# In each slot of the attention loop, the inverse's product moved to directly behind the scores, the maxima behind it

## The chip, the cores and the metric

The kernel runs on one core of a Trainium2 chip. The time is the device time of one execution in microseconds (us). Each engine (TensorE or PE, VectorE or DVE, ScalarE or ACT, GpSimd or POOL) works through its own list of instructions, and semaphores hold an instruction back until what it needs is done. SyncE (SP) issues the transfers. Matmul results go to PSUM, whose eight banks are shared out by hand in this kernel.

## The reference

One mixer layer of a diffusion backbone, 2048 latent tokens behind 256 context tokens, width 1024. One projection feeds two groups of heads, whose outputs are gated, concatenated, projected and added to the residual:

```python
rw_l, _ = rwkv_branch(rwkv_prep(u_sh, *rw_p), ctx_states, ...)   # RWKV-7: a delta-rule state, both directions
k, v = mla_keys_values(u_mla, kv_g, w_ukv, rot)                  # 8 heads, low-rank keys and values
q = mla_queries(u_mla, q_g, w_uq, rot)
o = block_attention(q, concat([k, kc]), concat([v, vc]))         # softmax over 2304 keys
x = x + gate * (concatenate([rw_l, o * silu(g_mla)]) @ w_out)
return rms_norm(x, final_g)
```

## The kernel before

The kernel has an input phase (projections, until about 1000 us), a short phase for queries, keys and values, and then the loop that the change touches, `attention`, from 1186 us to the end. It runs 16 **jobs**, one for each pair of heads and tile of 512 queries (`hp`, `qt`). A job has nine **macros** (`m` = 0 to 8), a macro four **slots** (`j` = 0 to 3) and a fifth call `side(4)` without scores. A slot does this on PE, in this order:

- **scores**: three matmuls of 512 columns (L1438 to L1440) into one buffer `bs`; ACT takes the exponential of it (L1442, tile `pt`), POOL adds that to `acc` (L1447);
- **maxima** for the next job's softmax: none to five matmuls (L1318) of 512 or 256 columns, each into a `bs` buffer of its own, each reduced on DVE to one column (L1319, tile `m`). They are handed out by a budget of columns (`due`, `rate`) in macros 1 to 7, and the list is emptied in macro 8;
- **side(j)**: while the RWKV branch lasts, `rw.slot`, which takes the inverse of one chunk one step on. A step is a product of 8 to 17 small matmuls (L328, L331, L334) into a `bx` buffer and its eviction on DVE or ACT. In slot 3 of every third macro `rw.slot` also issues the transposes of a chunk (L287). When the branch is done, `side` calls `late`, which issues steps of the output phase (`post`, `out_tiles`), most of them DVE work.

`bs` has three PSUM banks, which scores and maxima share, and `bx` two. Behind the four slots a macro issues the product with the values (`pv`, L1465, eight matmuls) and a larger piece of the RWKV branch (`tiled`). By the macro's number modulo 3 that is `chain1` and the next scores of the branch (L407, L308, L417; macros 0, 3, 6), `chain2` (L433; macros 1, 4, 7) or `chain3` and `chain4` (L447, L463; macros 2, 5, 8).

`chain2` needs the tile `Rf`, the inverse's last eviction (L394, DVE). Ahead of it on DVE stands the scaling of the next chunk's keys (L251, tile `x`): SP loads `x` behind the scores of `chain1` (L245), ACT takes two exponentials of it (L247, L248), then DVE multiplies (L251).

PE's order is the order in which the code is written (`manual_schedule` for PE). The orders of DVE, ACT, POOL and SP, and which of the three banks a `bs` tile gets, are set when the program is built, by a scheduler that estimates when each operation becomes ready; on the chip they are fixed. Jobs 0, 1, 2, 4, 5, 6, 8 and 9 are alike up to the names of the banks (called regular below). Jobs 3 and 7 prepare maxima for another pair of heads, with keys of 256 columns from a buffer `kx`. The branch ends in job 10; jobs 11 to 15 run `late`.

Of the kernel before, what the change touches and what calls it, by code (L numbers as in the profile page):

```python
# [468 lines left out]
class Kern:  # L469
# [864 lines left out]
    def attention(self, top, es, right, k, q, load_q, maxima, sets, pieces):  # L1334
        nc, tc, rw = self.nc, self.tc, self.rw
        L, CT, NT = self.L, self.CT, self.NT
        QW = min(512, L)
        NQ, NK, NQS = L // QW, NT // P, QW // P
        KW, NP = 512, len(pieces)
        kp = es.enter_context(tc.tile_pool(name="kp", bufs=1))  # L1340
        sets[1] = es.enter_context(tc.tile_pool(name="qb", bufs=1))
        pp = es.enter_context(tc.tile_pool(name="pp", bufs=2))

        KS, VS = [], []
        for j, (o, w) in enumerate(pieces):
            kt = kp.tile([97, 2, 2, w], F32R, name=f"kt{j}")
            for e in range(2):
                nc.sync.dma_start(kt[64:97, e].bitcast(F32), self.s_krr[:, :, o:o + w].rearrange("s p t -> p s t"))
            KS.append(kt)
            VS.append(kp.tile([P, w // P, P], F32, name=f"vt{j}"))  # L1350

        def load_kv(hp, j):
            o, w = pieces[j]
            for e in range(2):
                nc.sync.dma_start(KS[j][0:64, e].bitcast(F32),
                                  self.s_kn[:, hp, 64 * e:64 * e + 64, o:o + w].rearrange("s p t -> p s t"))
            nc.sync.dma_start(VS[j], self.s_vm[o:o + w, hp * P:(hp + 1) * P].rearrange("(j p) c -> p j c", p=P))

        def finish(hp, qt, oo, acc, last):

            cols = slice(qt * QW, (qt + 1) * QW)
            ob = pp.tile([P, QW], F32, name="ob", bufs=1)
            nc.scalar.copy(ob, oo)
            yield 1
            dn = self.bank("s")
            for e in range(2):
                nc.tensor.matmul(dn[64 * e:64 * e + 64, 0:QW], self.ones[:, 0:64], acc[e], start=True, stop=True)
            gr = pp.tile([P, 2, QW], F32, name="gr", bufs=1)
            g, rc = gr[:, 0], gr[:, 1]
            nc.scalar.copy(rc, dn[:, 0:QW])  # L1370
            nc.sync.dma_start(g, self.s_g[4 + hp][:, cols])
            yield 1
            for c in range(0, QW, P):
                nc.vector.reciprocal(rc[:, c:c + P], rc[:, c:c + P])
                yield 1
            nc.gpsimd.tensor_tensor(ob, ob, g, op=ALU.mult)
            nc.gpsimd.tensor_tensor(ob, ob, rc, op=ALU.mult)
            yield 1
            hl = pp.tile([P, 2, QW], F32, name="gr", bufs=1).bitcast(F32R)
            nc.scalar.copy(hl[:, 0], ob)  # L1380
            nc.gpsimd.tensor_tensor(hl[:, 1], ob, hl[:, 0].bitcast(F32), op=ALU.subtract)
            if last:
                self.hl = hl
            else:
                nc.sync.dma_start(self.s_mix[:, 4 + hp, :, cols].rearrange("s p t -> p s t"), hl.bitcast(F32))
            yield 2

        jobs = [(hp, qt) for hp in range(4) for qt in range(NQ)]
        for j in range(NP):
            load_kv(0, j)  # L1390
        NM = NK // 2
        macros = len(jobs) * NM
        rest = 5 * max(1, macros - (rw.total - k))
        fin, prev = iter(()), None

        def side(j):

            nonlocal prev
            if k < rw.total:
                rw.slot(5 * k + j)  # L1400
            else:
                self.late(rest)
            if m > 0 and next(fin, None) == 2:
                hp_, qt_ = prev
                prev = None
                if hp_ == 3:
                    if qt_ < NQ - 1:
                        self.outs.append(self.out_tiles(qt_))
                    if qt_ == NQ - 2 or NQ == 1:
                        self.outs.append(self.out_tiles(NQ - 1))  # L1410

        for ji, (hp, qt) in enumerate(jobs):
            nxt = jobs[ji + 1] if ji + 1 < len(jobs) else None
            mg = iter(())
            if nxt:
                nq = load_q(*nxt)
                mg = maxima(nq, nxt[0], KS if nxt[0] == hp else None, sets[1], "kx", 256)
            oo = self.bank("o", QW)
            acc = [pp.tile([P, QW], F32, name=f"acc{e}") for e in range(2)]
            held = {}  # L1420
            due = 0.0

            share = [self.MAXIMA[(k + i) % 3] if k + i < rw.total else 1 for i in range(1, NM - 1)]
            rate = [0] + [2 * NQS * NT * x / (4 * sum(share)) + 8 for x in share] + [0]
            for m in range(NM):
                if k < rw.total:
                    rw.begin(k)
                elif self.post_ is None:
                    right.close()
                    self.post_ = self.post(top)  # L1430
                pts = {}
                if m == 0:
                    next(mg, None)
                for j in range(4):
                    kt, e = 2 * m + j // 2, j % 2
                    ks, sl = KS[kt * P // KW], slice(kt * P % KW, kt * P % KW + P)
                    ps = self.bank("s", QW)
                    nc.tensor.matmul(ps, ks[:, e, 0, sl], q[:, e, 0], start=True, stop=False)  # L1438
                    nc.tensor.matmul(ps, ks[:, e, 0, sl], q[:, e, 1], start=False, stop=False)  # L1439
                    nc.tensor.matmul(ps, ks[:, e, 1, sl], q[:, e, 0], start=False, stop=True)  # L1440
                    pt = pp.tile([P, QW], F32, name=f"pt{e}", bufs=3)
                    nc.scalar.activation(pt, ps, AF.Exp, scale=SCALE)  # L1442
                    pts[kt, e] = pt
                    if kt == 0:
                        held[e] = pt
                    else:
                        nc.gpsimd.tensor_tensor(acc[e], held[e] if kt == 1 else acc[e], pt, op=ALU.add)  # L1447
                    if 1 <= m < NM - 1:
                        due += rate[m]
                        while due > 0:  # L1450
                            due -= next(mg, 1e9)
                    elif m == NM - 1 and j == 1:
                        for _ in mg:
                            pass
                    side(j)
                side(4)

                def pv():
                    if m == 0:

                        next(fin, None)
                    for kt in (2 * m, 2 * m + 1):
                        j, i = kt * P // KW, kt % (KW // P)
                        for e in range(2):
                            nc.tensor.matmul(oo[64 * e:64 * e + 64], VS[j][:, i, 64 * e:64 * e + 64], pts[kt, e],  # L1465
                                             start=kt == 0, stop=kt == NK - 1)
                        if nxt and nxt[0] != hp and (kt == NK - 1 or (kt + 1) % (KW // P) == 0):
                            load_kv(nxt[0], j)

                if k < rw.total:  # L1470
                    rw.tiled(k, pv)
                    k += 1
                else:
                    pv()

            fin, prev = finish(hp, qt, oo, acc, nxt is None), (hp, qt)
            next(fin)
            if nxt:
                q = nq
        while k < rw.total:  # L1480
            rw.begin(k)
            for j in range(5):
                rw.slot(5 * k + j)
            rw.tiled(k)
            k += 1
        if self.post_ is None:
            right.close()
            self.post_ = self.post(top)
        if not self.outs and NQ == 1:
            self.outs.append(self.out_tiles(0))  # L1490
        for _ in fin:
            pass
# [212 lines left out]
```

## Time and profile before

| | us |
|---|---|
| median of 3 runs | 2980.08 |
| lowest, highest | 2977.0, 3002.14 |
| profiled execution | 2988.63 |
| its span (first to last instruction) | 2986.9 |

The profiled execution is 8.55 us above the median, and 1.7 us of it lie outside the span. PE is busy for 90% of the span, DVE for 61%, POOL for 46%, ACT for 43%. A busy PE isn't PE at its peak, since matmuls overlap and their ends are modelled. In a row of the timeline the first number is the start in us from the span's beginning, the second the duration of the group in us; brackets hold the idle time of the engine just before, and who ended it.

### The profile page before, as it was taken

How to read it: one execution, taken by the hardware profiler on the slowest of the kernel's cores; microseconds unless marked ns; L12 is line 12 of the kernel's file. 1: busy time of each engine (PE TensorE's matmuls, PEld its weight loads, DVE VectorE, ACT ScalarE, POOL GpSimd, SP SyncE). 2: the span in 40 equal slices, each digit the busy share in tenths (PEclk: the TensorE clock that was granted, in tenths of full speed). 3: DMA queues.
4: the chain of work that ended last, by engine and by line, in shares of the span. 5: the costliest groups of instructions: out<-in, count | busy, mean ns of one | idle time of the engine just before them, and what ended most of it. 6: DMA issues, size and time to landing. Idle time of an engine off the chain costs nothing.

```text
span 2986.9 us, 55082 instructions
## 1 busy us (share of the span) xinstructions
PE 2692.9 (90%) x22035; PEld 2052.6 (69%) x22035; DVE 1817.3 (61%) x2832; ACT 1287.5 (43%) x2245; POOL 1387.9 (46%) x1220
## 2 busy tenths in 40 slices
PE   5999999998898898999998999898899977888998
PEld 3898899987788787666665666566666644445776
DVE  3347844357623566777766777765777668997213
ACT  3448744346633432445444444444444432332221
POOL 2323322323332122666565666565666556776332
PEclk7999999999999998999999999999999978889999
DMA  5225552225554876322133222133222044444443
GB/s 202 79 88 131 137 167 88 84 86 140 147 157 156 270 224 170 77 72 73 59 107 88 61 72 65 57 98 90 70 74 63 26 138 132 114 127 116 149 130 120
DMA packets 409466, 336.66 MB, mean 113 GB/s; under 512 B 130598, under 2 KB 341841, under 8 KB 408185
## 3 DMA queue, kind: packets, MB, share of 16 engines
q1 hardware_dynamic: 405775, 327.19, 37.4%
q8 instruction: 173, 2.83, 0.4%
q0 software_dynamic: 992, 3.21, 0.3%
q10 hardware_dynamic: 2442, 2.73, 0.3%
q14 instruction: 84, 0.69, 0.1%
HBM read 210.68 MB, written 122.31 MB: 111 GB/s over the span
## 4 chain that ended last, share of the span: by engine, by line
PE 65%; DVE 16%; DMA 6%; ACT 6%; issue 3%; POOL 3%; SPq 1%; ACTq 0%; POOLq 0%; DVEq 0%
PE pm L117 18%; PE bo L1465 7%; PE bx L1622 6%; PE bs L1438 5%; DVE m L1319 3%; PE bs L1440 3%; PE bs L1439 3%; PE bs L1318 3%; PE bx L331 3%; DMA x<-s_x 3%; PE bc L407 2%; ACT pt L1442 2%; DVE x L251 2%; PE bs L1108 2%; PE bx L433 1%
## 5 line engine op out<-in xcount | busy, mean ns | idle before, releaser
L1447 POOL TENSOR_TENSOR acc<-acc,pt 128x512 f32<-128x512 f32 x512 | 663.4, 1310 | 571.4 <-ACT pt L1442 566.9
L1442 ACT ACTIVATE pt<-bs 128x512 f32<-128x512 f32 x576 | 342.8, 597 | 513.2 <-PE bs L1440 484.1
L1319 DVE TENSOR_REDUCE m<-bs 128x1 f32<-128x512 f32 (+1 forms) x736 | 400.3, 568 | 176.4 <-PE bs L1318 172.6
L1438 PE MATMUL bs<-q,kt 97*128 97x512 f32 x576 | 280.6, 487 | 44.1 <-DVE m L1319 26.1
L1465 PE MATMUL bo<-pt,vt 128*64 128x512 f32 x1152 | 299.1, 643 | 0.0
L549 POOL TENSOR_TENSOR wlo<-wraw,whi 128x1024 fp32r<-128x1024 f32 (+1 forms) x56 | 133.9, 2392 | 294.7 <-PE pm L117 213.0
L1318 PE MATMUL bs<-kt,q 96*128 96x512 f32 (+1 forms) x480 | 181.5, 407 | 67.5 <-ACT pt L1442 28.3
L1440 PE MATMUL bs<-q,kt 97*128 97x512 f32 x576 | 236.4, 410 | 0.0
L1439 PE MATMUL bs<-q,kt 97*128 97x512 f32 x576 | 236.0, 410 | 0.0
L1438 PEld LDWEIGHTS bs<-q,kt 97*128 97x128 f32 x576 | 112.4, 195 | 121.1 <-DVE m L1319 36.3
L1318 PEld LDWEIGHTS bs<-kt,q 96*128 96x128 f32 x480 | 91.1, 190 | 134.3 <-ACT pt L1442 62.3
L132 ACT COPY u<-pm 128x342 f32<-128x342 f32 (+1 forms) x168 | 74.1, 441 | 210.2 <-PE pm L117 209.7
L1465 PEld LDWEIGHTS bo<-pt,vt 128*64 128x64 f32 x1152 | 76.7, 146 | 120.2 <-issue 113.1
L1440 PEld LDWEIGHTS bs<-q,kt 97*128 97x128 f32 x576 | 113.5, 197 | 27.0
L1622 PE MATMUL bx<-wohi,big 128*128 128x512 f32 x496 | 126.0, 394 | 3.9 <-DMA big<-s_mix 3.9
L1439 PEld LDWEIGHTS bs<-q,kt 97*128 97x128 f32 x576 | 114.4, 199 | 4.6
L1622 PEld LDWEIGHTS bx<-wohi,big 128*128 128x128 f32 x496 | 93.7, 190 | 25.2 <-issue 4.9
L1658 DVE TENSOR_TENSOR acc<-bx,big 128x512 f32<-128x512 f32 x32 | 22.1, 690 | 143.2 <-PE bx L1622 128.5
L371 DVE TENSOR_TENSOR R<-bx,R 128x512 f16<-128x512 f32 x108 | 73.6, 682 | 57.7 <-PE bx L331 56.7
L826 DVE SCALAR_TENSOR_TENSOR kd<-z,u 128x512 f32<-128x512 f32 x32 | 38.9, 1219 | 111.3 <-ACT z L824 111.3
L348 DVE TENSOR_TENSOR bdg<-bx,lvl 64x512 f16<-64x512 f32 x144 | 98.7, 685 | 5.2 <-PE bx L331 2.3
L331 PEld LDWEIGHTS <-bdg 128*128 128x128 f16 x1728 | 67.9, 100 | 44.6 <-issue 41.4
(320 smaller groups left out, 6363.4 us busy)
## 6 DMA issues: line engine op xcount, KB each, us to landing
wraw<-in_w_in SPq DMA_DIRECT2D x54, 512.0 KB
x<-s_x SPq DMA_DIRECT2D x72, 384.0 KB
s_x<-xt SPq DMA_DIRECT2D x32, 512.0 KB
big<-s_mix SPq DMA_DIRECT2D x24, 512.0 KB
s_kn<-hl SPq DMA_DIRECT2D x36, 256.0 KB
ar<-s_nr SPq DMA_DIRECT2D x72, 128.0 KB
uv<-s_v SPq DMA_DIRECT2D x72, 128.0 KB
s_x<-cum SPq DMA_DIRECT2D x32, 256.0 KB
```

Of the source, the lines that this page charges most:

```text
L117: nc.tensor.matmul(ps[0:m, 0:w], a[:, k, 0:m], x[:, k], start=n == 0, stop=n == 3 * KT - 1)
L331: nc.tensor.matmul(ps[:, h], lhsT[:, h], r, start=plus is None, stop=also is None and (plus is None or h == 7))
L549: (eng_lo or nc.vector).tensor_tensor(lo, x, hi.bitcast(F32), op=ALU.subtract)
L1318: nc.tensor.matmul(ps[:, 0:w], q[0:96, e, 0, i * P:(i + 1) * P], ks[e], start=True, stop=True)
L1319: nc.vector.tensor_reduce(m5[:, e * NQS + i, j:j + 1], ps[:, 0:w], axis=AX.X, op=ALU.max)
L1438: nc.tensor.matmul(ps, ks[:, e, 0, sl], q[:, e, 0], start=True, stop=False)
L1439: nc.tensor.matmul(ps, ks[:, e, 0, sl], q[:, e, 1], start=False, stop=False)
L1440: nc.tensor.matmul(ps, ks[:, e, 1, sl], q[:, e, 0], start=False, stop=True)
L1442: nc.scalar.activation(pt, ps, AF.Exp, scale=SCALE)
L1447: nc.gpsimd.tensor_tensor(acc[e], held[e] if kt == 1 else acc[e], pt, op=ALU.add)
L1465: nc.tensor.matmul(oo[64 * e:64 * e + 64], VS[j][:, i, 64 * e:64 * e + 64], pts[kt, e], start=kt == 0, stop=kt == NK - 1)
L1622: nc.tensor.matmul(ps, x[:, i], a[:, k, 512 * h:512 * h + 512], start=n == 0, stop=n == last)
```

## The change

In each slot the call `side(j)` moves from the end of the slot to directly behind the scores, so that the inverse's product (or a step of `late`) is issued ahead of that slot's maxima. `side(4)` stays where it is. Nothing is added or left out.

```diff
                         nc.gpsimd.tensor_tensor(acc[e], held[e] if kt == 1 else acc[e], pt, op=ALU.add)
+                    side(j)
                     if 1 <= m < NM - 1:
                         due += rate[m]
                         while due > 0:
...
                     elif m == NM - 1 and j == 1:
                         for _ in mg:
                             pass
-                    side(j)
                 side(4)
```

Three places of the built program are shown, all in macro 7 of job 2. On PE, at slot 1, the long product of slot 0 (L334) stands last in its slot before:

```order
L334 MATMUL bx<-T_15373,bdg_8168 128x64
L1438 MATMUL bs<-q,kt_11415 128x512
L1439 MATMUL bs<-q,kt_11415 128x512
L1440 MATMUL bs<-q,kt_11415 128x512
L1318 MATMUL bs<-kt_11419,q 128x256 x2
L331 LDWEIGHTS bdph_8160
L331 MATMUL bx<-T_15388,bdph_8160 128x64
```

and in the changed program, where the place shown is the end of slot 1 and the start of slot 2 (the product of slot 1, its maxima, the scores of slot 2, and that slot's product at once):

```order
L331 MATMUL bx<-T_15388,bdph_8160 128x64
L1318 MATMUL bs<-kt_11419,q 128x256 x2
L1438 MATMUL bs<-q,kt_11415 128x512
L1439 MATMUL bs<-q,kt_11415 128x512
L1440 MATMUL bs<-q,kt_11415 128x512
L328 LDWEIGHTS idt
L328 MATMUL bx<-lvl,idt 128x512
```

The maxima now touch the scores of the next slot, and the product stands between a slot's scores and its maxima.

On DVE, from the first maxima of the macro to `Rf` (pm, bdf and bdg are the inverse's evictions, m the maxima's), before:

```order
L1319 TENSOR_REDUCE m_14321<-bs 128x1
L353 TENSOR_TENSOR pm_15425<-bdph_8162,lvl 128x1024
L1319 TENSOR_REDUCE m_14321<-bs 128x1 x3
L342 CAST bdf<-bx 64x8x64
L1319 TENSOR_REDUCE m_14321<-bs 128x1
L348 TENSOR_TENSOR bdg_8166<-bx,lvl 64x8x64 x2
L251 TENSOR_TENSOR x<-x 128x4x128 x2
L1319 TENSOR_REDUCE m_14321<-bs 128x1 x2
L394 TENSOR_TENSOR Rf<-bx,R_15211 128x512
L1322 TENSOR_REDUCE mx<-m_14321 128x8
```

and in the changed program:

```order
L353 TENSOR_TENSOR pm_15425<-bdph_8162,lvl 128x1024
L1319 TENSOR_REDUCE m_14321<-bs 128x1 x3
L342 CAST bdf<-bx 64x8x64
L348 TENSOR_TENSOR bdg_8166<-bx,lvl 64x8x64 x2
L251 TENSOR_TENSOR x<-x 128x4x128 x2
L1319 TENSOR_REDUCE m_14321<-bs 128x1 x4
L1322 TENSOR_REDUCE mx<-m_14321 128x8
L394 TENSOR_TENSOR Rf<-bx,R_15211 128x512
```

All maxima of slot 0 are now reduced behind L353, and those of slot 1 behind L251 as well as those of slot 2: four reductions stand between L251 and `Rf` instead of two.

On ACT, in the same macro, the exponentials of slots 1, 2 and 3 (pt) around those of the next chunk (L247, L248), before:

```order
L1442 ACTIVATE pt_15507<-bs 128x512
L247 ACTIVATE e<-x 128x8x64
L1442 ACTIVATE pt_15531<-bs 128x512
L248 ACTIVATE x<-x 128x8x64
L359 CAST T_15552<-bx 128x512
L1442 ACTIVATE pt_15558<-bs 128x512
```

and in the changed program:

```order
L1442 ACTIVATE pt_15507<-bs 128x512
L247 ACTIVATE e<-x 128x8x64
L248 ACTIVATE x<-x 128x8x64
L1442 ACTIVATE pt_15531<-bs 128x512
L359 CAST T_15544<-bx 128x512
L1442 ACTIVATE pt_15558<-bs 128x512
```

Slot 2's exponential moved behind L248. It is so in every macro 1, 4 and 7 of the changed program from macro 4 of job 0 on.

## Rows read from the trace of the kernel before

**Rows 1.** Stretches of 100 us: busy us of PE, PEld, DVE, ACT, POOL; clock; DMA

```profile
1400.00:1500.00 100.00, 91.97 (x1105) 63.83 (x1103) 73.90 (x112) 48.40 (x86) 61.93 (x60) 1.00 0.25 72
...
2600.00:2700.00 100.00, 85.17 (x300) 43.92 (x298) 93.21 (x131) 35.44 (x61) 75.49 (x53) 0.87 0.36 103
```

**Rows 2.** Waits of PE, 1181 to 2375 us: us in total, times, longest

```profile
PE bs L1318 <- ACT pt L1442: 37.2, 65, 1.4
PE bx L433 <- DVE Rf L394: 16.0, 14, 4.4
PE bs L1318 <- DVE m L1319: 13.0, 25, 1.0
PE bx L331 <- DVE R L371: 5.8, 16, 1.1
```

**Rows 3.** Timeline of macro 7, job 2, by engine

```profile
1491.10 0.50 PE L1438 MATMUL bs<-q,kt 97*128 97x512 f32 x1
...
1492.56 0.68 DVE L353 TENSOR_TENSOR pm<-bdph,lvl 128x1024 f16<-128x1024 f16 x1
...
1496.23 0.63 ACT L247 ACTIVATE e<-x 128x512 f32<-128x512 f32 x1 [0.65 <-DMA x<-s_x]
...
1496.77 0.58 ACT L1442 ACTIVATE pt<-bs 128x512 f32<-128x512 f32 x1
...
1497.24 0.62 ACT L248 ACTIVATE x<-x 128x512 f32<-128x512 f32 x1
1497.40 0.50 PE L1438 MATMUL bs<-q,kt 97*128 97x512 f32 x1
...
1497.90 1.80 DVE L251 TENSOR_TENSOR x<-x 128x512 f32<-128x512 f32 x2 [0.22 <-ACT x L248]
...
1498.99 1.94 PE L1465 MATMUL bo<-pt,vt 128*64 128x512 f32 x8
...
1499.72 0.76 DVE L1319 TENSOR_REDUCE m<-bs 128x1 f32<-128x256 f32 x2
1500.39 0.68 DVE L394 TENSOR_TENSOR Rf<-bx,R 128x512 f32<-128x512 f32 x1
...
1501.22 1.15 PE L433 MATMUL bx<-bt,Rf 64*64 64x64 f32 x32 [0.30 <-DVE mx L1322]
```

**Rows 4.** Timeline of macro 4, job 2, by engine

```profile
1453.99 0.50 PE L1438 MATMUL bs<-q,kt 97*128 97x512 f32 x1
...
1457.55 0.50 PE L1318 MATMUL bs<-kt,q 96*128 96x512 f32 x1 [0.66 <-ACT pt L1442]
...
1459.57 0.63 ACT L247 ACTIVATE e<-x 128x512 f32<-128x512 f32 x1 [1.10 <-DMA x<-s_x]
...
1464.95 1.15 PE L433 MATMUL bx<-bt,Rf 64*64 64x64 f32 x32 [0.52 <-DVE Rf L394]
```

**Rows 5.** Timeline of macro 1, job 2, by engine

```profile
1416.15 0.50 PE L1438 MATMUL bs<-q,kt 97*128 97x512 f32 x1
...
1418.36 0.75 DVE L353 TENSOR_TENSOR pm<-bdph,lvl 128x1024 f16<-128x1024 f16 x1 [0.27 <-ACT bdph L316]
...
1422.33 0.48 PE L1438 MATMUL bs<-q,kt 97*128 97x512 f32 x1
...
1423.20 2.32 DVE L251 TENSOR_TENSOR x<-x 128x512 f32<-128x512 f32 x2
...
1424.16 0.50 PE L1318 MATMUL bs<-kt,q 96*128 96x512 f32 x1 [0.65 <-ACT pt L1442]
...
1428.18 1.15 PE L433 MATMUL bx<-bt,Rf 64*64 64x64 f32 x32 [0.96 <-DVE Rf L394]
```

**Rows 6.** Macro 1 of job 6: PE's timeline, then a stretch of 2 us

```profile
1874.73 0.50 PE L1318 MATMUL bs<-kt,q 96*128 96x512 f32 x1 [1.00 <-ACT pt L1442]
...
1876.04 3.39 PE L1465 MATMUL bo<-pt,vt 128*64 128x512 f32 x8
...
1876.00:1878.00 2.00, 2.00 (x9) 0.73 (x8) 1.99 (x4) 0.59 (x1) 2.00 (x4) 0.50 0.00 0
```

## The prediction

> **What bounds the kernel now.** I read the stretches first. In the steady part of the loop PE is busy 92 of 100 us at the full clock (2.4 GHz, shown as 1.00) and DVE only 74; in jobs 11 to 14 DVE is busy 93 of 100 us and PE 85 [rows 1]. So the loop hangs on PE up to about 2375 us, then on DVE, and at the end on PE's output matmuls. Next come PE's waits in the first part: 37.2 us in 65 waits of maxima for an exponential, 13.0 us for a reduction, 16.0 us of `chain2` for `Rf`, 5.8 us of a product for its predecessor R [rows 2]. The first two are waits for one of the three `bs` banks. They are what an order of PE can change, and together with the 5.8 us they limit any gain to 56 us.
>
> Then the timelines of the macros that end in `chain2`. In all three DMA, ACT and DVE form one chain: `x` lands, L247, L248, L251, a few reductions, `Rf`, `chain2`; PE arrives there 0.30 to 0.96 us early [rows 3 to 5]. PE thus has less than a microsecond to give away there, and what PE waits for at those places decides.
>
> **The change part by part.** No instruction is added. The product is issued one to three maxima earlier; the maxima lose the product that stood between them and the next scores. I replayed the macros of a regular job by hand, in the order of the built program, with the durations of the rows; times below count from the macro's first scores.
>
> *Macro 7.* Before, `x` lands so that L247 starts at 5.13 (1496.23 less 1491.10), and slot 3's scores start at 6.30 [rows 3]. Changed, slot 1's two maxima are reduced behind L251. With slot 2's scores they hold all three banks. Slot 2's first maximum must wait for the exponential of its own slot, which stands behind L247 and L248: 5.13 + 0.63 + 0.62 + 0.58 = 7.0. Its second one waits for the first reduction behind L251: L251 starts at 6.5, ends at 8.3 (1.80), and one of two reductions in 0.76 us makes 8.7. Slot 3's scores wait for the next, 9.05. From there on PE runs as before: 1.59 to `pv` (1497.40 to 1498.99) and 1.87 to its end, so that `chain2` starts at 12.5. `Rf` isn't late for that: two more reductions and 0.2 + 0.68 end at about 10.6. Before it was 10.12. **+2.4 us.**
>
> *Macro 4.* L247 starts at 5.58 [rows 4]. Here slot 3's scores wait for slot 2's exponential, again behind L248: 5.58 + 1.83 = 7.4. Their maximum waits for the slot's own exponential, which takes 1.8 us from scores to release (1422.33 to 1424.16 [rows 5]): 9.2. A product and `pv` make 0.7 + 1.87: `chain2` at 11.8 against 10.96. **+0.9 us.**
>
> *Macro 1.* Slot 1's scores must wait for the first reduction, which now stands behind L353: 2.21 + 0.75 + 0.69 = 3.65. Slot 3's scores wait for slot 2's exponential until 7.4 instead of 6.18, and the last maximum for a reduction behind L251, 6.8 + 2.32 + 0.69 = 9.8; the rest makes 12.4 against 12.03, since `chain2` had waited 0.96 us for `Rf` anyway [rows 5]. **+0.3 us** (0 to 0.5, as L251 takes 1.80 or 2.32).
>
> *Macros 3 and 6* hold a slot without a product; there a maximum still waits for its own scores' exponential, now 0.9 us once where before it was about 0.57 (37.2 over 65) twice [rows 2]: **-0.3 us** for both together, as the first wait of such a macro comes out longer by a little. *Macro 5*: R is evicted ahead of the slot's reductions, so the wait for R goes, 5.8 over 16: **-0.3 us** [rows 2]. Macros 0, 2 and 8 have few or no maxima and little idle: 0, hidden behind PE's own work.
>
> A regular job gains 3.0 us in length, eight of them **24 us**. Each macro's term is good to about half a microsecond, so 12 to 36. Jobs 3 and 7 already stand with reductions behind L251; I take 0, between -4 and +4 for both. In jobs 11 to 14 a step of `late` goes ahead of the maxima on DVE; DVE's sum is the same and it is the bound [rows 1], so 0, give or take 5. POOL's acc additions swap places with the scaling of `ar`, and on SP a gate load moves ahead of two key loads; POOL is busy 62% there, and neither is waited for at these places: 0.
>
> *The clock.* By the same replay the waits of PE add up to 3.3 to 4.7 us in each of macros 1, 4 and 7, bunched in 6 to 8 us. In macro 1 of job 6 a wait of 1.00 us in place of the usual 0.65 was followed by a granted clock of 0.50 (1.2 GHz), and `pv` took 3.39 us where it takes 1.94 [rows 3, 5, 6]. The waits I expect are longer, so I count a fall of the clock in each of these macros. Its price is 0 where the slow stretch lies under the next wait, and 1.45 where it holds `pv`; no row shows one at the place where mine begins, so I take 1.1, nearer to the `pv` row as most of the waits stand shortly ahead of `pv`. Three a job, eight jobs: **26 us**, between 0 and 35.
>
> The Trainium skill (TensorE: Matmul & The Clock Gate, A second HAM failure mode: psum-queue depth-cycling) says that a PE which idles briefly again and again while its matmuls cycle through PSUM banks swings between the two clocks. That speaks against this change; row and rule agree on the sign, and it gives no price.
>
> Sum: 24 + 26 = 50 us on the profiled execution's 2988.6, 3039 us. That execution is 8.55 us above the median, so against the median of 2980 I expect **3030 us**.
>
> **The rivals.**
>
> *Waits without the clock.* The new waits come, but the clock stays up: 2980 + 24 = 3004 us, 2992 to 3016. For it: macro 1 of job 2 has several waits, one of 0.65 us and 0.96 at its end, and `pv` between them runs at its usual pace. Against it: rows 6, with hardly more idle time. The same page (section HAM oscillation — how this bites in real kernels) ties a fall to one unbroken gap without matmuls; by that rule the gaps of 0.4 to 1.6 us that I replay would lower nothing and this rival would hold. The trace disagrees: the longest wait ahead of the fall in rows 6 is 1.00 us.
>
> *Faster.* The product fills the time in which a maximum waits for an exponential. Price: the 37.2 and the 5.8 us go, 2980 - 43 = 2937 us. It decides in macro 7: if `x` lands before slot 1's maxima are issued, that is before about 4 us instead of 5.13, L251 no longer holds the reductions and the banks come free in time. For it: 65 of the waits are of this kind [rows 2]. Against it: L247 waited 0.65 and 1.10 us for the transfer of `x` in these macros [rows 3, 4], so `x` is late already, and nothing moves its issue forward.
>
> *Nothing.* Waits change places, and as PE has slack ahead of `Rf` in a `chain2` macro, the sum stays: 2980 us, within 12. For it: macro 1, where it comes out nearly so. Against it: in macro 7 slot 3's scores start 2.75 us later and PE had 0.30 us to spare.
>
> **How the numbers follow.** Forecast 0.52, waits without the clock 0.23, nothing 0.13, faster 0.12. A measurement of this kernel can tell about 1%, 30 us, from no change. The forecast reaches from 3008 (24 + 4) to 3060 (36 + 35 and a little for jobs 3, 7 and 11 to 14). For 8 times in 10 the range takes in the second rival and the upper half of nothing: 2978 to 3062. Slower by over 1% (above 3010): 0.48 of the forecast and 0.08 of the second case, 0.56. Faster by over 1%: 0.10. Within 1%: 0.34.
>
> **What would show it.** In the profile after, `chain2` should start 12.5 us or more behind the first scores of macro 7 in a regular job instead of 10.1, in macro 4 about 11.8 or more instead of 11.0, and macros 3, 5 and 6 should be no longer than before. Maxima (L1318) and scores (L1438) should wait for DVE's L1319 and for the exponential just behind L248, more than the 56 us of before; `chain2` should hardly wait for `Rf`. The granted clock should show stretches at 0.5 shortly ahead of or in `pv` in these macros. I am wrong if L1318's waits shrink, if the clock stays at 1.00, or if the time is lost in jobs 11 to 15.

## The result and the profile after

The changed kernel takes 3065.25 us (median of 6 runs), the kernel before 2993.08 (6 runs beside them): ratio **1.0284, interval 1.0258 to 1.031**. It is slower, by more than the range allowed for. The two medians by themselves stand 72 us apart (1.0241); costs below are reckoned with the ratios on record, which make it 85 us. The profiled execution of the changed kernel took 3080.77 us, 92.1 more than that of before; its span is 3079.0.

First two stretches of 100 us that answer to [rows 1], same columns, in the changed kernel; the second one begins at 2700 because everything late now stands some 75 us further back:

```profile
1400.00:1500.00 100.00, 92.53 (x1086) 62.36 (x1085) 70.50 (x108) 45.66 (x81) 59.06 (x56) 0.97 0.25 72
2700.00:2800.00 100.00, 81.70 (x270) 42.69 (x271) 83.90 (x125) 31.68 (x56) 69.29 (x50) 0.81 0.38 111
```

PE looks as busy as before in the steady part (92.53 for 91.97), but its granted clock is 0.97 instead of 1.00. In the late jobs DVE is at 84 of 100 instead of 93.

To see where the 92 us are, I cut both traces at the first scores of jobs. The kernel before, columns as in [rows 1]: jobs 0 to 2, 4 to 6 and 8 to 9 (the eight regular ones), then jobs 3 and 7, then jobs 11 to 14:

```profile
1186.84:1512.06 325.22, 301.61 (x3555) 208.17 (x3553) 229.22 (x352) 155.57 (x277) 203.88 (x195) 0.99 0.28 73
1636.54:1968.40 331.86, 304.60 (x3591) 208.87 (x3589) 237.54 (x357) 157.62 (x282) 205.82 (x198) 0.98 0.23 66
2093.84:2311.96 218.12, 201.53 (x2395) 138.87 (x2394) 155.71 (x238) 105.40 (x188) 137.36 (x132) 0.99 0.23 67
...
1512.06:1636.54 124.48, 109.90 (x1232) 76.64 (x1231) 82.48 (x156) 53.58 (x95) 72.14 (x68) 0.95 0.36 101
1968.40:2093.84 125.44, 112.24 (x1232) 79.30 (x1231) 81.92 (x156) 53.31 (x95) 72.06 (x68) 0.92 0.35 100
...
2402.68:2785.86 383.18, 311.03 (x1139) 176.85 (x1135) 305.74 (x462) 121.44 (x211) 240.80 (x175) 0.87 0.45 130
```

The changed kernel, the same jobs in the same order:

```profile
1176.64:1522.04 345.40, 316.75 (x3556) 210.84 (x3554) 230.11 (x352) 156.24 (x277) 203.03 (x195) 0.94 0.27 69
1661.44:2013.51 352.07, 322.41 (x3591) 212.22 (x3589) 233.66 (x357) 158.41 (x281) 205.37 (x197) 0.93 0.21 62
2152.55:2385.79 233.24, 214.18 (x2395) 141.91 (x2394) 155.24 (x238) 105.95 (x188) 136.66 (x132) 0.93 0.21 63
...
1522.04:1661.44 139.40, 119.19 (x1232) 81.66 (x1231) 83.50 (x156) 54.01 (x95) 72.09 (x68) 0.86 0.31 90
2013.51:2152.55 139.04, 117.88 (x1233) 81.57 (x1231) 83.57 (x156) 53.73 (x95) 71.88 (x68) 0.86 0.31 89
...
2478.82:2878.00 399.18, 324.02 (x1139) 181.59 (x1135) 304.09 (x462) 120.94 (x211) 241.75 (x175) 0.83 0.43 125
```

With the same matmuls in each piece, a longer busy time is in the main a slower clock, and what is left is waiting. (The clock column bears this out for the regular jobs: what it lacks to 1.00, times the length, rises by about 50 us over the three rows, an estimate from the rounded clocks.) Regular jobs: 875.20 to 930.71 us, **+55.5**, of which PE's busy time is +45.6 (807.74 to 853.34) and its idle time +9.9. Jobs 3 and 7: 249.92 to 278.44, **+28.5**, +14.9 busy and +13.6 idle. Jobs 11 to 14: **+16.0**, +13.0 busy and +3.0 idle. Job 10 adds 2.3, and 10.2 come off ahead of the first job (1186.84 to 1176.64); together 92.1. The 10.2 are not the change's: in the kernels of the experiments the first scores come anywhere from 1168.2 to 1183.3 us, in either order.

PE's waits in jobs 0 to 10, columns as in [rows 2]: first two of the kernel before, which [rows 2] does not show, then those of the changed kernel:

```profile
PE bs L1438 <- ACT pt L1442: 7.0, 17, 0.5
PE bs L1438 <- DVE m L1319: 5.5, 7, 1.8
```

```profile
PE bs L1318 <- ACT pt L1442: 38.8, 63, 2.3
PE bs L1318 <- DVE m L1319: 29.2, 36, 1.9
PE bs L1438 <- DVE m L1319: 28.3, 16, 4.8
PE bs L1438 <- ACT pt L1442: 18.4, 41, 1.3
```

The waits of maxima for exponentials are as before, those of maxima for reductions have gone from 13.0 to 29.2, the scores' own waits from 5.5 to 28.3 and from 7.0 to 18.4, and `chain2`'s wait for `Rf` is gone [rows 2]. So is most of the wait for R, 2.1 us instead of 5.8.

Macro 7 of job 2 in the changed kernel, the timeline that answers to [rows 3]:

```profile
1495.82 0.50 PE L1438 MATMUL bs<-q,kt 97*128 97x512 f32 x1
...
1501.13 0.63 ACT L247 ACTIVATE e<-x 128x512 f32<-128x512 f32 x1 [0.83 <-DMA x<-s_x]
...
1502.46 1.93 DVE L251 TENSOR_TENSOR x<-x 128x512 f32<-128x512 f32 x2 [0.49 <-ACT x L248]
...
1502.97 0.38 PE L1318 MATMUL bs<-kt,q 96*128 96x256 f32 x1 [1.18 <-ACT pt L1442]
...
1504.42 1.52 DVE L1319 TENSOR_REDUCE m<-bs 128x1 f32<-128x256 f32 x4
...
1504.90 0.58 PE L1318 MATMUL bs<-kt,q 96*128 96x256 f32 x1 [1.55 <-DVE m L1319]
...
1505.28 0.75 PE L1438 MATMUL bs<-q,kt 97*128 97x512 f32 x1
...
1508.12 3.24 PE L1465 MATMUL bo<-pt,vt 128*64 128x512 f32 x8
...
1511.29 1.15 PE L433 MATMUL bx<-bt,Rf 64*64 64x64 f32 x32
```

Four reductions stand behind the two scalings, one maximum waits 1.18 us for an exponential, the next 1.55 us for a reduction, and slot 3's scores come 9.46 us behind the first ones. From there until past 1510 us PE runs at half pace: `pv` takes 3.24 us, `chain2` starts at 15.47. The same macro in stretches of 2 and 4 us, clock third from the end, and then whole, with macro 4 of job 2 ahead of it and macro 4 of job 5 behind:

```profile
1502.00:1504.00 2.00, 0.38 (x1) 0.19 (x1) 1.54 (x2) 1.39 (x3) 2.00 (x4) 0.99 0.00 0
1504.00:1506.00 2.00, 1.10 (x3) 0.96 (x4) 1.92 (x6) 0.00 (x0) 2.00 (x4) 0.50 0.00 0
1506.00:1510.00 4.00, 4.00 (x26) 1.88 (x26) 0.87 (x2) 1.18 (x2) 2.22 (x2) 0.50 0.01 4
1510.00:1512.00 2.00, 2.00 (x30) 0.83 (x28) 0.00 (x0) 0.00 (x0) 0.00 (x0) 0.80 0.00 0
...
1456.17:1471.53 15.36, 13.33 (x112) 7.37 (x108) 8.66 (x13) 7.70 (x14) 8.71 (x10) 0.78 0.24 72
1495.82:1512.37 16.55, 13.13 (x115) 7.57 (x111) 8.51 (x16) 7.71 (x14) 8.74 (x10) 0.79 0.22 68
1833.59:1845.48 11.89, 10.55 (x113) 6.18 (x109) 8.21 (x13) 7.70 (x14) 8.24 (x10) 1.00 0.29 92
```

The kernel before, macro 7 of job 2 and macro 4 of job 2:

```profile
1491.10:1502.29 11.19, 10.26 (x114) 6.67 (x110) 8.08 (x16) 7.59 (x14) 7.54 (x10) 1.00 0.35 101
1453.99:1465.99 12.00, 10.09 (x112) 6.20 (x108) 8.59 (x13) 7.50 (x14) 8.25 (x10) 1.00 0.31 92
```

In macro 7 idle time went from 0.93 to 3.42 us, +2.5, and busy time from 10.26 to 13.13, +2.9. In macro 4 idle time hardly moved; where the clock fell (jobs 2, 4, 6 and 9) it lasts 14.3 to 15.9 us, where it did not, 11.9 to 12.3, as long as before. (PE is busy for 10.55 us there, in job 5, where job 2 had 10.09 before, both at a clock of 1.00: not quite all of a longer busy time is the clock.) In the regular jobs the clock is under 1.00 in all eight macros 7, in four macros 4 and in six macros 1. Of these 18 places two, macros 1 and 4 of job 6, were under 1.00 before.

### The profile page after: what moved, and what is told of

It reads as the page before. It is cut to its first block, busy times and chain, and to the rows that moved or that the text cites. A ratio compares the mean times of both kernels' runs of the same rounds, so it can differ in the third digit from the quotient of the medians.

```text
span 3079.0 us, 55061 instructions
## 1 busy us (share of the span) xinstructions
PE 2764.6 (90%) x22035; PEld 2068.8 (67%) x22035; DVE 1815.2 (59%) x2832; ACT 1289.5 (42%) x2245; POOL 1387.8 (45%) x1220
## 4 chain that ended last, share of the span: by engine, by line
PE 67%; DVE 11%; DMA 8%; ACT 6%; issue 4%; POOL 3%; SPq 1%; ACTq 0%; POOLq 0%; DVEq 0%
PE pm L117 18%; PE bo L1465 9%; PE bx L1622 6%; PE bs L1438 5%; PE bs L1318 4%; PE bs L1440 3%; PE bs L1439 3%; PE bx L331 3%; DMA x<-s_x 3%; ACT pt L1442 2%; PE bc L407 2%; PE bs L1108 2%; DVE x L251 1%; DVE m L1319 1%; PE bx L433 1%
## 5 line engine op out<-in xcount | busy, mean ns | idle before, releaser
L1438 PE MATMUL bs<-q,kt 97*128 97x512 f32 x576 | 283.2, 492 | 80.4 <-DVE m L1319 49.8
L1465 PE MATMUL bo<-pt,vt 128*64 128x512 f32 x1152 | 320.4, 683 | 0.0
L1318 PE MATMUL bs<-kt,q 96*128 96x512 f32 (+1 forms) x480 | 196.6, 449 | 85.4 <-ACT pt L1442 36.4
L1440 PE MATMUL bs<-q,kt 97*128 97x512 f32 x576 | 244.4, 424 | 0.0
L1439 PE MATMUL bs<-q,kt 97*128 97x512 f32 x576 | 243.2, 422 | 0.0
L1438 PEld LDWEIGHTS bs<-q,kt 97*128 97x128 f32 x576 | 115.6, 201 | 182.9 <-ACT pt L1442 65.6
L1440 PEld LDWEIGHTS bs<-q,kt 97*128 97x128 f32 x576 | 118.1, 205 | 29.0
L1439 PEld LDWEIGHTS bs<-q,kt 97*128 97x128 f32 x576 | 118.6, 206 | 7.7
L348 DVE TENSOR_TENSOR bdg<-bx,lvl 64x512 f16<-64x512 f32 x144 | 98.8, 686 | 11.0 <-PE bx L331 6.1
```

The costliest lines, as they stand in the source:

```text
L1318: nc.tensor.matmul(ps[:, 0:w], q[0:96, e, 0, i * P:(i + 1) * P], ks[e], start=True, stop=True)
```

## Experiments

My theory: reductions that stand behind the scaling L251 on DVE keep PE's banks, PE waits in bunches, and the clock falls. Rivals: maxima next to scores cost wherever they stand; or the loss sits in the jobs that I had put at zero.

**One stretch at a time.** Two kernels set the new order by the place (`ahead` stands for `side(j)` ahead of the maxima, otherwise behind):

```
e1_branch_only:  ahead = k < rw.total      # jobs with a right chain
e2_late_only:    ahead = k >= rw.total     # jobs 11 to 15
```

> The move only while the RWKV branch lasts (jobs 0 to 10); from then on the old order. If all of the loss comes from the branch's macros (reductions and slot 2's exponential behind the scaling of the next chunk's keys), this is as slow as the full change: 70 to 85 us above the kernel before. If what the profile after shows in jobs 11 to 14 (109, 89, 89 and 112 us against 106, 82, 86 and 108, some 16 us) belongs to the move itself, it is 55 to 70 us above. If the loss comes from maxima standing next to scores as such, it lies in between by the share of macros, about 55.

> The complement: the move only in the macros behind the branch (jobs 11 to 15), where side issues steps of the output phase. If the move costs there by itself: 10 to 18 us above the kernel before. If the 16 us in the profile after are only the clock's state, carried over or by chance: within 5 us of the kernel before.

The first gave **1.0278** (1.025 to 1.0305), the second **1.0071** (1.0049 to 1.0093). The jobs with a right chain (the RWKV branch, jobs 0 to 10) carry most of it, 83 us, and the late jobs cost about 21 us by themselves, which I had put at zero. Together that is 104, more than the 85 of the whole; the intervals only just meet. A macro of the second kernel that lasts 13.9 us where it took 7.3 (macro 5 of job 12) shows how a loss comes about there; timeline of PE and DVE, first before, then in the second kernel:

```profile
2559.33 0.50 PE L1438 MATMUL bs<-q,kt 97*128 97x512 f32 x1
...
2560.57 1.29 DVE L1319 TENSOR_REDUCE m<-bs 128x1 f32<-128x512 f32 x2
```

```profile
2546.80 1.16 DVE L1588 TENSOR_TENSOR big<-big,acc 128x512 f32<-128x512 f32 x1
...
2547.88 1.76 DVE L1563 TENSOR_TENSOR big<-big 128x512 f32<-128x512 f32 x1
...
2549.56 1.75 DVE L1572 TENSOR_TENSOR acc<-acc,bon 128x512 f32<-128x512 f32 x1
...
2551.23 1.96 DVE L1319 TENSOR_REDUCE m<-bs 128x1 f32<-128x512 f32 x3
...
2551.96 0.49 PE L1318 MATMUL bs<-kt,q 96*128 96x512 f32 x1 [2.42 <-DVE m L1319]
...
2557.22 3.60 PE L1469 MATMUL bo<-pt,vt 128*64 128x512 f32 x8
```

Three steps of the late work now come ahead of the first reduction; a maximum waits 2.42 us for it, and `pv` then runs at half pace. It is macro 7 again with another instruction in L251's place. Summed over jobs 11 to 14, however, PE's waits for reductions hardly grow: 32.7 us before, 35.6 in this kernel, 33.7 in the changed one. The macro is an example; it does not show that all of the 21 us come about in this way.

**Is it a DVE instruction that waits?** This kernel is the one with the late jobs alone, each late step cut where DVE would wait in it:

```
  for b in range(4): nc.tensor.transpose(...)
+ yield 1
  ...
- self.split(hl[:, 0], hl[:, 1], mx)
+ nc.scalar.copy(hl[:, 0], mx)
+ yield 1
+ nc.vector.tensor_tensor(hl[:, 1], mx, hl[:, 0].bitcast(F32), op=ALU.subtract)
```

> The changed order in jobs 11 to 15 alone, as in the run that gave 1.0071, but each late step is cut where DVE would wait inside it: the product that follows the transposes, and the subtraction that follows the cast on ACT, come one step later (13 steps a tile instead of 11, paced so that they are spread over the same time). If the loss there is that reductions stand behind a DVE instruction which waits for ACT or PE, the loss goes: 0.999 to 1.004 of before. If it is the late steps' DVE time ahead of the reductions as such, 1.006 to 1.010 remains.

**1.0061** (1.004 to 1.0082): the loss stays, as in the second case. That does not rule out the first one, because the loss has changed its form. Over jobs 11 to 14 PE's busy time is back at 309.5 us (311.0 before, 320.0 with the late jobs alone), and its idle time is 93.2 (72.2 and 76.3); PE's waits for the load of the next queries alone rise from 12.5 to 21.6. The split thus took the slow clock away and brought waiting of its own. Whether it is the DVE time of the late steps ahead of the reductions, as the rows above suggest, was not shown.

**The scaling out of the way.** The changed kernel with L251 kept back and written behind the values' product:

```
- for d in range(2): nc.vector.tensor_tensor(self.bk[:, d], self.bk[:, d], cum...)
+ self.scaling = cum       # issued in tiled(), behind pv, where m % 3 == 1
```

> The full change, with the scaling of the next chunk's keys on DVE (L251) written behind the values' product of macros 1, 4 and 7 instead of one macro earlier, so that most reductions of the macro come ahead of it. If the reductions behind L251 are the cause, most of the loss in the branch goes: macro 7 of a regular job back from 15.5 to 17 us to about 12 to 13, the whole within 10 to 35 us above the kernel before. If maxima next to scores are the cause whatever DVE's order, it stays at 60 to 85 us above.

**1.0041** (1.002 to 1.0062): 2.4 of the 2.8% are gone, though not all of that is the change's, as the next run shows. In the regular jobs the scaling now stands behind the reductions that come ahead of `Rf`, in macros 4 and 7 with one of its two halves still ahead of `Rf`; in macros 1 and 4 of jobs 3 and 7 both halves stand ahead of `Rf` and of two reductions. Macro 7 of job 2 in it (maximum L1325, reduction L1326, scores L1445, scaling L264):

```profile
1478.42 0.63 ACT L250 ACTIVATE x<-x 128x512 f32<-128x512 f32 x1
1478.71 0.76 DVE L1326 TENSOR_REDUCE m<-bs 128x1 f32<-128x256 f32 x2
...
1479.59 0.51 PE L1325 MATMUL bs<-kt,q 96*128 96x256 f32 x2 [1.10 <-ACT pt L1449]
1479.93 0.40 PE L1445 MATMUL bs<-q,kt 97*128 97x512 f32 x1
...
1481.43 1.94 PE L1472 MATMUL bo<-pt,vt 128*64 128x512 f32 x8
```

The two reductions now start while L250 still runs, the wait for the exponential stays (1.10), the second one is gone, slot 3's scores come at 7.40 instead of 9.46, and `pv` has the full clock. (Slot 2's exponential still stands behind L250 on ACT, as the change has put it; no run moved that alone.) The regular jobs are back at 107 to 111 us. Jobs 3 and 7 are not: 126.2 and 137.8, where 124.5 and 125.4 were before.

**The same without the change.** The kernel before with the same edit:

> The kernel before, with the scaling L251 moved behind Rf on DVE and nothing else. It tells whether the scaling is a burden in the old order too. Before, chain2 waits 16.0 us for Rf, 14 times, and Rf stands behind the scaling. If these waits were a loss of their own, they go and the kernel is 10 to 16 us faster, 2961 to 2967. If something else is due at the same time (the exponentials or the reductions behind the scaling), it is within 6 us of before.

**0.9878** (0.9854 to 0.9902), more than twice the gain that I had expected, 36 us against the 16.0 of waits for `Rf`, which are gone. Macros 1 and 4 last 12.3 and 11.1 us (medians of the regular jobs) where they took 13.1 and 11.9; jobs 3 and 7 last 119.8 and 118.3. With the scaling late in both orders the change thus costs 1.0041 / 0.9878 = 1.0165, against 1.0284 with it in place: some 1.2 of the 2.8% hang on L251, and 1.6 stay without it.

**Both parts taken away.** The new order in the jobs with a right chain, the scaling late:

> The new order in the jobs with a right chain only, jobs 11 to 15 in the old one, and the scaling moved behind Rf. The two parts found so far are taken away together. If the loss is the scaling ahead of the reductions plus the late steps ahead of the maxima, what remains is jobs 3 and 7, which were 1.7 and 12.4 us longer than before with the scaling late, less what regular jobs gain: 2970 to 2992. If the parts are not additive, it stays at 2990 or above.

**1.0003** (0.9981 to 1.0024). Beside the run before it, the new order costs 1.3% even with L251 late: jobs 3 and 7 are 9 and 10 us longer than there, jobs 10 and 11 are 7 and 8, regular jobs between 2 us shorter and 5 longer. Job 11 has the old order in both, so a few us of such differences are scatter between two executions. The regular jobs together lose 10.4 us (861.6 to 872.0), where with the scaling in place they lost 55.5: in them L251 is the greater part of the cause. In jobs 3 and 7 nearly all of the difference lies in macros 1 and 4, 3.3 to 5.3 us in each. Macro 1 of job 3 in this kernel:

```profile
1524.14 1.41 DVE L355 TENSOR_TENSOR bdg<-bx,lvl 64x512 f16<-64x512 f32 x2
...
1525.58 1.08 DVE L1326 TENSOR_REDUCE m<-bs 128x1 f32<-128x256 f32 x3
...
1526.06 0.79 PE L1445 MATMUL bs<-q,kt 97*128 97x512 f32 x1 [1.74 <-DVE m L1326]
```

All three reductions of slot 1 stand behind the inverse's evictions (L355, L348 in the kernel before), and slot 2's scores wait 1.74 us for them, 1.41 in macro 4; in the run before, all three stand ahead of L355 and these scores do not wait. So this is DVE's order once more, with the evictions of the product that was moved forward in L251's place. (The scaling follows at 1526.70 and is done before the next reductions are due.) No run moved the evictions, so this is read from the timeline; that maxima next to scores cost wherever they stand is not shown by this run.

**By macro.** The new order only outside the macros that end in `chain2`; and only in macro 7 of the regular jobs:

```
e3_not_chain2:    ahead = k < rw.total and m % 3 != 1
e11_macro7_only:  ahead = k < rw.total and m == 7 and not wide    # wide: jobs 3 and 7
```

> The new order only in macros 0, 2, 3, 5, 6 and 8 of the jobs with a right chain; macros 1, 4 and 7, the ones that end in chain2, and jobs 11 to 15 keep the old order. My theory is that the loss sits where a DMA-fed scaling (L251) stands ahead of the reductions, which is in macros 1, 4 and 7 alone: then a regular job keeps its old 11.2 to 12 us in macro 7 and gains about 1 us in macros 2, 3, 5 and 6, and the whole is 0 to 12 us faster than the kernel before, 2965 to 2977. Rival: the order hurts wherever a maximum stands next to scores, or any saved microsecond is taken back by the next wait; then it is over 2985.

> The changed order in macro 7 of the regular jobs alone, eight places in all. My prediction had 2.4 us of waits and 1.1 of clock for each, 28 us. The trace after has this macro at 15.5 to 17.0 us where it was 11.2, with the granted clock at 0.79 to 0.89 over it; by those lengths the same eight places cost 35 to 46 us: 3015 to 3026 where the kernel before is 2980. If the waits are made by the neighbours (macro 6 ends earlier, macro 8 takes up what is left), it is under 3008.

The first: **0.9973** (0.995 to 0.9995), a gain of 8 us. Regular macros 3, 5 and 6 are 0.2 to 0.5 us shorter and most regular jobs 0.4 to 2.2, but jobs 3 and 7 are 5.8 and 3.1 longer, above all in macros 3 and 6 of job 3 (17.9 and 18.7 us for 15.7 each). The second: **1.0131** (1.0092 to 1.0169), 39 us from eight places; macro 7 lasts 15.0 to 16.9 us there, and in job 2 its idle time is 3.42 us, to the digit that of the fully changed kernel:

```profile
1485.95:1501.49 15.54, 12.12 (x114) 7.08 (x110) 8.53 (x16) 7.71 (x14) 8.74 (x10) 0.89 0.23 70
```

**By job.** The new order in the regular jobs alone, and in jobs 3 and 7 alone:

> The changed order in the regular jobs alone: jobs 3 and 7, whose maxima take keys of the next pair of heads, and jobs 11 to 15 keep the old order; the scaling stays where it was. This prices the term for the regular jobs (24 us of waits and 26 of clock over eight of them) without the two that I took as 0. By the lengths of the jobs in the trace after (52 us over the regular jobs, 7 us won ahead of the first job, 28 us in jobs 3 and 7) it comes to 3015 to 3030. Rival: the regular jobs are hurt by what jobs 3 and 7 and the late jobs leave behind, or jobs 3 and 7 are no cost; then it is under 3005 or above 3045.

> The changed order in jobs 3 and 7 alone, everything else as before. My prediction had 0 for them, between -4 and +4 for both. By the lengths in the trace after they cost 28 us, by the difference of the two runs with the whole right chain and with the regular jobs alone 36: 3000 to 3020 where the kernel before is 2980. If they only inherit what regular jobs leave behind, they cost nothing here: within 10 us of before.

**1.0157** (1.0129 to 1.0185), 47 us, and **1.0101** (1.0066 to 1.0136), 30 us. With the 21 of the late jobs these make 98, where the whole change costs 85 (2.84% of 2993): the parts add up within their intervals, and the loop alone is 102.3 us longer in the trace. (Cut at the first scores of job 0, the 52 and 7 us of the expectation for the regular jobs are 55.5 and 10.2; their difference, on which it rests, is the same.) In jobs 3 and 7 slots have up to four maxima. Waits of PE's scores for reductions in job 3, kernel before, then changed:

```profile
PE bs L1438 <- DVE m L1319: 2.6, 3, 1.8
```

```profile
PE bs L1438 <- DVE m L1319: 8.0, 4, 3.8
```

The longest, 3.78 us, are slot 2's scores of macro 1, behind 2.31 us of L251 (timeline of the changed kernel):

```profile
1540.82 2.31 DVE L251 TENSOR_TENSOR x<-x 128x512 f32<-128x512 f32 x2
...
1543.64 0.80 PE L1438 MATMUL bs<-q,kt 97*128 97x512 f32 x1 [3.78 <-DVE m L1319]
```

**Work in the gaps.** The changed kernel with 272 more matmuls, whose result is overwritten, ahead of a product in macros 1, 4 and 7, so that PE has something to do before the waits:

```
+ for _ in range(self.fill):
+     nc.tensor.matmul(ps, self.idt, self.id8, start=True, stop=True)
```

> The full change with matmuls added that are overwritten at once: eight of 512 columns ahead of slot 2's product in macros 1, 4 and 7 of regular jobs, twelve ahead of slot 1's product in jobs 3 and 7 (272 in all, some 60 us of PE at the full clock, meant to lie in PE's waits). If the fall of the clock behind the waits makes more than half of the loss, the clock stays at 1.00 there, the values' product takes 1.9 us again instead of 3.2, and the time falls by 15 to 40 us against the full change in spite of the work added. If the waits alone make the loss, it is the same or up to 40 us slower than the full change.

**1.0267** (1.0237 to 1.0297). The clock came back, as in the first case, to 0.946 over the span (changed kernel 0.925, before 0.948), with five falls instead of 18 in macros 1, 4 and 7 of the regular jobs; the time is the changed kernel's, as in the second case. At the 0.23 us between starts that 512-column matmuls show at the full clock, 272 of them are 63 us of PE work. The 192 in regular jobs are 44, yet PE's busy time there rises by only 3.2 us (853.3 to 856.5): by this estimate the clock gave back some 41 us, and the filler took them. The run shows that the clock falls less often when PE has work in these gaps; no run shows the loss with the clock held up and nothing added.

**What pays.** The scaling late, and the new order in the regular jobs outside macros 1, 4 and 7:

> A candidate that takes what the runs so far show to pay: the scaling L251 behind Rf (1.2% by itself), and the new order in macros 0, 2, 3, 5, 6 and 8 of the regular jobs alone, not in jobs 3 and 7, not in the macros that end in chain2 and not late. If the two gains are independent, the regular jobs, which last 105 to 109 us with the scaling late alone, lose another 1 to 2 us each, and the whole is 2932 to 2948 where the kernel before is 2980. If one eats the other, because the clock falls that remain are set off by the same waits, it is level with the scaling alone, 0.984 to 0.992 of before.

**0.9856** (0.982 to 0.9892). This beats the kernel before and the changed one; its regular jobs last 104.3 to 108.3 us. Its interval overlaps that of the late scaling alone, so the gain is the scaling's, and what the order adds to it was not shown.

## Why the prediction was wrong

The direction was right, and so was the mechanism in the regular jobs; the time was 35 us too low, 3 us outside the range. (By the medians 13 of the 35 belong to the kernel before, 2993.08 beside the changed one where I had reckoned with 2980.08; by the ratio all 35 are the change's.) Three steps failed: the two terms that I put at 0, for jobs 3 and 7 and for jobs 11 to 14, which the trace has at 28.5 and 16.0 us, and the price of a fall of the clock. By the prediction's steps:

*The regular jobs: right as a sum, by luck.* I had 24 us of waits and 26 of clock, 50; the regular jobs alone measure 47, the trace says 55.5. But PE's idle time rose by 9.9 and its busy time by 45.6. The waits of *macro 7* were right, +19.1 us idle over eight for 19.2: slot 3's scores come at 9.46 for 9.05, slot 2's two maxima at 7.15 and 9.08 for 7.0 and 8.7. So were those of *macro 1*, +2.6 for 2.4. *Macro 4* has no waits to add where the clock stays up (11.9 to 12.3 us for 12.0); over eight its idle time fell by 4.4 where I had +7.2. *Macros 3, 5 and 6* gave back 9.0 us where I had 4.8. A slowed PE also arrives later and so may wait less, which would move time from the one term to the other.

*The clock: 1.1 us a fall was too little.* The step that failed is "Its price is 0 where the slow stretch lies under the next wait, and 1.45 where it holds `pv`". In macro 7 the clock stays at 0.50 from 1504 to past 1510 us and slows slot 3's scores and products too: +2.9 busy in the fully changed kernel, +1.9 with macro 7 alone (12.12 less 10.26). The falls were fewer than the 24 I counted, 18 in macros 1, 4 and 7; the busy time of these macros rose by 43.1 us, some 2.4 a fall. The fall in macro 7 follows waits of 1.18 and 1.55 us. The Trainium skill (TensorE: Matmul & The Clock Gate, section A second HAM failure mode: psum-queue depth-cycling) says that short idle times between groups of matmuls that cycle through PSUM banks make the clock swing; this trace agrees. By the section HAM oscillation — how this bites in real kernels of the same page of the Trainium skill, which speaks of one long gap, the fall in macro 7 would not have come; there the trace disagrees.

*Jobs 3 and 7: the step "I take 0, between -4 and +4 for both" failed.* They cost 28.5 us in the trace and 30 measured alone. I had argued that reductions stand behind L251 there already. They do, but with up to four maxima in a slot all banks hang on them once the product no longer stands between, and the next scores wait up to 3.8 us (1.8 before). With the scaling late the order still costs 9 to 10 us in each, and there the reductions stand behind the inverse's own evictions, which I had not considered. Which wait lengthens macros 3 and 6 of job 3 when the new order stands outside the `chain2` macros, where there is no L251, is open.

*Jobs 11 to 14: "DVE's sum is the same and it is the bound [rows 1], so 0, give or take 5" failed.* DVE's sum is the same (305.74 and 304.09), but a share of 93% in the stretch did not make it the bound of each macro. The loss is 13.0 us of a slower PE and 3.0 of idle time in the trace, 21 measured alone. In the macro shown, late steps ahead of the reductions keep the banks; what makes the whole of it stays open.

*Smaller things.* `chain2` no longer waits for `Rf` and R is evicted earlier, as forecast. No wait of PE names POOL; on SP's side the waits of maxima for the load of the next queries rose from 4.0 to 6.4 us in jobs 0 to 10, where I had 0. The cap of 56 us on a gain left out what scores waited for banks, 10.7 us over the same stretch. In macro 1 the 7.4 for slot 3's scores should have been 7.2 by the durations used beside it; the term does not rest on it. L247 started 5.31 us into macro 7, so *Faster* had no chance; *Waits without the clock* and *Nothing* fell with the clock.

## What to carry to other kernels

When instructions change places on the engine that fills PSUM banks, look at what stands on the draining engine between the fill and the drain: a DMA-fed or merely long instruction ahead of a reduction keeps the bank, and moving that instruction (L251 behind `Rf`, 1.2%) was worth more here than any order tried on PE. An engine busy 93% of a stretch is not thereby the bound of each step in it; a term of 0 there needs a replay like any other. And split a loss into PE's busy time and its idle time over the same matmuls, and hold the granted clock against it: that tells the clock from the waits. Before a part of a loss is put down to an instruction that was moved away, move it away in the old order too: here half of what was won by that had nothing to do with the change.

## What the runs showed of the chip

Two waits of 1.18 and 1.55 us, with one maximum between them, were followed by a granted clock of 0.50 (1.2 GHz) for over 6 us, through work without a gap (4.00 busy of 4.00 us from 1506 on). Over the regular jobs PE was busy 45.6 us longer, in the main by the slower clock, for 9.9 us of additional idle time. Macro 4 came out both ways with the same instructions, 4 falls in 8, so its length is near one of two values, and a mean describes neither.
